# Weight sums of a seven-product up-projection taken out of its loop, with a reordered product chain

## The chip, the cores and the metric

The kernel runs on one core of one Trainium2 chip. The core has five instruction streams that run on their own: TensorE (PE, with its weight loads listed as PEld), VectorE (DVE), ScalarE (ACT), GpSimd (POOL) and SyncE (SP), the last of which only issues transfers here. The metric is the device time of one execution in microseconds, as the median of several runs.

## The reference, cut to what matters

One layer of a streaming encoder over 2048 prompt tokens and 64 sample tokens, all in float32 with `D_MODEL = 1024` and `D_FF = 2816`:

```
x  = x + rms_norm(token_mixer(rms_norm(x)))        # gated convolution and mLSTM heads
x  = x + rms_norm(memory_attend(rms_norm(x)))      # 4 heads, 256 memory tokens
up, ff_new = causal_dwconv(rms_norm(x) @ w_up, ff_buf, ffn_conv_w)    # w_up: 1024 x 5632
a, g = split(up, 2)                                # each 2816 wide
x  = x + rms_norm((gelu(g) * a) @ w_down)
```

The results are `x` and the new states; among them `new_ffn_conv`, the last two rows of `rms_norm(x) @ w_up` of the prompt and of the sample (2 x 5632 numbers each).

## The kernel before, in words

Every float32 product is made of three matmuls on TensorE: an operand is split into a rounded high part and the remainder (`split`, lines 101 and 102: ACT writes the high part as a cast, DVE subtracts it from the source), and `mm3` (lines 115 to 117) adds high-high, high-low and low-high in PSUM. The five phases run one after another; a compile-time planner orders the instructions of each engine by simulated readiness, except on the engines named in `manual_schedule`, where the written order holds. In phases 3 to 5 this is PE.

**Attention stage (`phase3`, main loop from line 1142).** Sixteen chunks of 128 tokens. One iteration issues, in this order on PE: the scores of chunk i+1 (two halves), the transposes of the normalised result of chunk i-1 (`x2_T`, line 1184, whose DVE copies `xg` go to the DRAM tensor `x2Td`), the transposes of chunk i+2, the output product of chunk i in two halves (`yout`), and between them the transposes of the softmax of chunk i+1 (`pT`, line 1067). The residual `xr` of `yout` is loaded from DRAM into a tile with one buffer. After a chunk's output, `post` and `x2n` normalise it on ACT, DVE and POOL. The three `raw` buffers of 4 KB per partition are nearly unused in this loop.

**Up-projection stage (`phase4`, from line 1191).** Tokens go in 3 passes of 704, held as four quarter matrices R11, R12, R21, R22 (half of the 1024 rows by 352 tokens). In each pass a loop runs over 22 units; unit f makes the 128 columns f of the half `a` and the 128 columns f of the half `g`. As a 2 x 2 block product this would be eight block products; the kernel makes seven (the Winograd form of Strassen's scheme) out of sums of token quarters (T1 to T4, made once a pass) and sums of weight quarters (s14, s23, made in each unit). A block product is 12 matmuls of 128 x 352, so a unit is 84. In each unit:

- SP loads two weight blocks of 512 KB (`raw`, `wr`); POOL makes four sums of 128 x 512 from them (lines 1260, 1261, 1262, 1265); ACT and DVE split the operands wa (1024 columns), wb (1024), wc (1024) and wd (512) of the next unit.
- PE makes the products in the order wa·B11, wb·T2, wb·T3, wa·B21, wc·T1, wd·T4, wc·B22. The partial sums u2 and u3 are added on DVE (lines 1398, 1404); `cg` and `ca` collect the two column blocks (lines 1412, 1418, 1423, 1431). wa·B21 is accumulated onto wa·B11's PSUM bank, and wc·B22 onto wc·T1's, the latter after DVE has read wc·T1 (line 1418).
- `conv` (lines 1346 and 1348) runs the three taps on ACT and DVE, ACT applies gelu, DVE multiplies (line 1438), and POOL stores the result in the DRAM tensor `hd`. POOL also copies the two halo columns in front of each block and behind it (lines 1324, 1326, 1351, 1353, 1354).

When a pass ends, seven token operands (B11, B21, B22, T1 to T4; one buffer each, 128 x 1408) are split anew, each after its last product of the old pass. After the last unit, two transfers on SP write the halo columns out, `self.dma(self.o["ffc"][:, :, 0], halo)` and the same for `halos`, into an output of shape (128, 44, 2, 2): each run of consecutive numbers in DRAM is two floats long.

**Down-projection (`phase5`).** `load_h` loads `hd` back (tile `hr`, split to `hh`), the weights are split to `dh` and `dl`, and PE starts on line 115 with the tile `y`.

Of the kernel before, what the change touches and what calls it, by code (L numbers as in the profile page):

```python
# [7 lines left out]
F32 = mybir.dt.float32  # L8
# [6 lines left out]
P = 128  # L15
# [50 lines left out]
class Prog:  # L66
# [68 lines left out]
    def build(self):  # L135
        tc, nc = self.tc, self.nc
        with ExitStack() as es:
# [23 lines left out]
            self.hd = dt([NF, P, T], F32, name="hd")  # L161
            self.qT = dt([4, P, T], F32, name="qTd")
# [811 lines left out]
    def phase3(self):  # L974
# [8 lines left out]
        with ExitStack() as es:  # L983
# [67 lines left out]

            zq = self.zq = self.pool(self.qes, "zq", side="right")
# [69 lines left out]

            def yout(s):
                yos = []
                xr = zq.tile([P, D], F32, tag="xr", name="xr", bufs=1)
                self.dma(xr, self.x1[s.c * P:(s.c + 1) * P])
                for nh in range(2):
# [8 lines left out]
                    if nh == 1:  # L1136
                        self.post(wk, yos, self.gb3, xr, self.x2[s.c * P:(s.c + 1) * P], yn=self.yn3,
                                  junk=s.pp[:, 0:2].rearrange("p h m -> p (h m)"))
                        x2n(self.yn3, xr)
                        todo.append((xr, s.c * P, P))  # L1140
                    yield

            todo = self.x2todo = []
            ch = {0: xT(0)}
# [4 lines left out]
            for i in range(16):  # L1149
                g = score(ch[i + 1]) if i + 1 < 16 else iter(())  # L1150
                next(g, None)
                if i == 0:
                    pT(ch[0])
                next(g, None)
                while todo:
                    self.x2_T(pt_, "tp", *todo.pop(0))
# [3 lines left out]
                next(y)  # L1160
                next(y)
                if i + 1 < 16:
                    pT(ch[i + 1])
                next(y)
                next(y)
                if i == 1:
# [7 lines left out]
                    todo.append((xt, NP_TOK, W))  # L1174

# [14 lines left out]
    def phase4(self):  # L1190
# [6 lines left out]

        tc, nc, a = self.tc, self.nc, self.a
        V, G = nc.vector, nc.gpsimd
# [4 lines left out]
        with ExitStack() as es:  # L1204
# [13 lines left out]


            ops = {n: t_op(n) for n in ("B11", "T2")}  # L1220
            raws = {n: t_raw(n) for n in ("R11", "R12", "R21", "R22")}
            wa0 = left.tile([P, 2, KT, P], F32R, tag="wa", name="wa0", bufs=1)
            wb = left.tile([P, 2, 2, KH, P], F32R, tag="wb", name="wb", bufs=1)
            X = early.tile([P, KH, NB], F32, tag="X", name="X", bufs=1)
            s23 = early.tile([P, 2, KH, P], F32, tag="s23", name="s23", bufs=1)
            s14 = early.tile([P, 2, KH, P], F32, tag="s14", name="s14", bufs=1)
            zq2 = self.zq
            halo = right.tile([P, 2 * NF, 2], F32, name="halo")
            halos = right.tile([P, 2 * NF, 2], F32, name="halos")
            G.memset(halo, 0.0)  # L1230
            self.dma(halos, a["sffn"])
# [6 lines left out]
            def w_load(u):  # L1238
                w = W()
                f = units[u][1]  # L1240
                w.r0 = self.raw(a["w_up"][f], (P, KT, P))
                w.r1 = right.tile([P, KT, P], F32, tag="wr1", name="wr1", bufs=2)
                self.dma(w.r1, a["w_up"][NF + f])
                return w

            def w_a(u, w):
                if u == 0:
                    w.a = wa0
                else:
                    w.a = (right if u % 2 else left).tile([P, 2, KT, P], F32R, tag="wa", name="wa", bufs=1)  # L1250
                self.split(w.a[:, 0], w.a[:, 1], w.r0)

            def w_s123(u, w):
                if u == 0:
                    w.s14, w.s23 = s14, s23
                else:
                    w.s14 = early.tile([P, 2, KH, P], F32, tag="s14", name="s14", bufs=1)
                    w.s23 = early.tile([P, 2, KH, P], F32, tag="s23", name="s23", bufs=1)
                a11, a21, a22 = w.r0[:, 0:KH], w.r1[:, 0:KH], w.r1[:, KH:KT]
                G.tensor_tensor(out=w.s14[:, 0], in0=a21, in1=a22, op=ALU.add)  # L1260
                G.tensor_tensor(out=w.s23[:, 0], in0=w.s14[:, 0], in1=a11, op=ALU.subtract)
                G.tensor_tensor(out=w.s23[:, 1], in0=a11, in1=a21, op=ALU.subtract)

            def w_s4(w):
                G.tensor_tensor(out=w.s14[:, 1], in0=w.r0[:, KH:KT], in1=w.s23[:, 0], op=ALU.subtract)

            def w_b(u, w):
                w.b = wb if u == 0 else left.tile([P, 2, 2, KH, P], F32R, tag="wb", name="wb", bufs=1)
                self.split(w.b[:, 0], w.b[:, 1], w.s23)

            def w_c(w):
                w.c = left.tile([P, 2, 2, KH, P], F32R, tag="wc", name="wc", bufs=1)
                self.split(w.c[:, 0], w.c[:, 1], w.s14)

            def w_d(w):
                w.d = left.tile([P, 2, KH, P], F32R, tag="wd", name="wd", bufs=1)
                self.split(w.d[:, 0], w.d[:, 1], w.r1[:, KH:KT])
# [26 lines left out]
            def t_t3(p, t):  # L1304
                V.tensor_tensor(out=t.r["R11"], in0=t.X, in1=t.r["R11"], op=ALU.subtract)
                t_split(p, t, "T3", t.r["R11"])

            def t_t4(p, t):
                V.tensor_tensor(out=t.X, in0=t.X, in1=t.r["R21"], op=ALU.subtract)
                t_split(p, t, "T4", t.X)  # L1310

            def prod(pt, wh, wl, o, more=False):
                self.mm3(pt[:, :NB], [(wh[:, k], wl[:, k], o[:, k, 0], o[:, k, 1]) for k in range(KH)],
                         first=not more, more=more)
# [4 lines left out]
            def vt(n):  # L1319
                return left.tile([P, NB], F32, tag=n, name=n, bufs=1)  # L1320

            def cbuf(j, p, n):
                c = left.tile([P, 2 * NB + 4], F32, tag=n, name=n, bufs=1)
                G.tensor_copy(c[:, 0:2], halo[:, j])
                if p == NPASS - 1:
                    G.tensor_copy(c[:, NPL + 2:NPL + 4], halos[:, j])
                return c
# [14 lines left out]
            def conv(j, p, c, n, bufs):  # L1342
# [7 lines left out]
                if p < NPASS - 1:  # L1350
                    G.tensor_copy(halo[:, j], c[:, 2 * NB:2 * NB + 2])
                else:
                    G.tensor_copy(halo[:, j], c[:, NPL:NPL + 2])
                    G.tensor_copy(halos[:, j], c[:, 2 * NB + 2:2 * NB + 4])
                return d, e


            tk = t_load(0)
            w = w_load(0)
            t_split(0, tk, "B11", tk.r["R11"])  # L1360
            w_a(0, w)
            t_adds(tk)
            w_s123(0, w)
            t_split(0, tk, "T2", tk.X)
            w_b(0, w)
            t_t3(0, tk)
            t_split(0, tk, "B21", tk.r["R21"])
            w_s4(w)
            t_split(0, tk, "T1", tk.r["R12"])
            w_c(w)  # L1370
            t_t4(0, tk)
            w_d(w)
            t_split(0, tk, "B22", tk.r["R22"])
            ws = {0: w, 1: w_load(1)}
            nt = None
            for u, (p, f) in enumerate(units):
                w, n = ws.pop(u), ws.get(u + 1)
                if u + 2 < len(units):
                    ws[u + 2] = w_load(u + 2)
# [6 lines left out]
                pa = ptile()  # L1386
                prod(pa, w.a[:, 0, 0:KH], w.a[:, 1, 0:KH], o["B11"])
                p1 = vt("p1")
                nc.scalar.copy(p1, pa[:, :NB])
                if last:  # L1390
                    t_split(p + 1, nt, "B11", nt.r["R11"])
                if n:
                    w_s123(u + 1, n)
                    w_a(u + 1, n)
# [240 lines left out]
```

## Time and profile before

| | |
|---|---|
| median of 3 runs | 3039.05 us (3037.79 to 3041.55) |
| profiled execution | 3042.33 us, of it 3040.6 us span |
| granted clock of TensorE, mean over the span | 0.974 of 2.4 GHz |
| attention loop | about 1074 to 1488 us |
| up-projection, first to last matmul | 1491.7 to 2473 us |
| down-projection, first matmul to the end | 2527.7 to 3040.6 us |

How to read it: the span is the time from the first to the last instruction; the profiled execution lies 3.3 us above the median of the timed runs. Times below are microseconds from the start of the span. A bracket at the end of a timeline row gives how long the engine was idle just before the instruction, and what released it.

### The profile page before, as it was taken

The numbers are of one execution on the slowest core, as the hardware profiler recorded it, in microseconds if no ns is written. First come the engines' busy times: TensorE is split into PE (matmuls) and PEld (weight loads), VectorE is DVE, ScalarE is ACT, GpSimd is POOL, SyncE is SP. The second block draws the span as 40 slices with busy tenths as digits, with TensorE's granted clock in tenths as the row PEclk, the third lists the DMA queues.
The fourth block names the chain that finished last, engine by engine and source line by source line (L and its number), as shares of the span: only waits on it lengthen the run. The fifth ranks groups of instructions, "written<-read, shape, count | busy, mean of one in ns | idle before, by whom it ended". The sixth has DMA issues, their size and how long they took to land.

```text
span 3040.6 us, 41676 instructions
## 1 busy us (share of the span) xinstructions
PE 2873.7 (95%) x15906; PEld 2645.1 (87%) x15906; DVE 1856.3 (61%) x2771; ACT 1121.8 (37%) x1979; POOL 1057.6 (35%) x1177
## 2 busy tenths in 40 slices
PE   8999999999999999999689998999899957999998
PEld 8999999998888777888589997999899956888887
DVE  5313421446665544444589999999999951444449
ACT  5233223235443533333344554455444423211113
POOL 1111111112212201111368786778688830000016
PEclk9999999999999999999899998999899978999999
DMA  8434232258665423222432323232222374222126
GB/s 272 142 107 134 92 107 86 69 169 291 218 210 163 141 71 104 84 84 84 141 108 96 110 102 117 101 107 98 87 101 94 106 41 103 78 78 83 51 73 216
DMA packets 172042, 358.78 MB, mean 118 GB/s; under 512 B 31046, under 2 KB 96776, under 8 KB 171842
## 3 DMA queue, kind: packets, MB, share of 16 engines
q1 hardware_dynamic: 149666, 279.63, 30.7%
q0 software_dynamic: 22176, 76.48, 6.8%
q8 instruction: 125, 2.05, 0.3%
q14 instruction: 75, 0.61, 0.1%
HBM read 270.58 MB, written 85.47 MB: 117 GB/s over the span
## 4 chain that ended last, share of the span: by engine, by line
PE 45%; DVE 12%; issue 5%; ACT 2%; SPq 1%; DMA 1%; POOL 0%; DVEq 0%; ACTq 0%; POOLq 0%
PE up L115 6%; PE up L116 6%; PE up L117 6%; PE y L116 4%; PE y L117 4%; PE y L115 4%; DVE da L1348 2%; PE yo L116 2%; PE yo L117 2%; PE yo L115 2%; PE sc L117 2%; PE sc L115 2%; PE sc L116 2%; DVE acc L566 1%; SPq L71 1%
## 5 line engine op out<-in xcount | busy, mean ns | idle before, releaser
L115 PE MATMUL y<-dh,hh 128*128 128x512 f32 x704 | 275.0, 391 | 54.2 <-ACT dh L101 54.2
L116 PE MATMUL y<-dl,hh 128*128 128x512 f32 x704 | 275.0, 391 | 0.5 <-DVE dl L102 0.5
L117 PE MATMUL y<-dh,hh 128*128 128x512 f32 x704 | 274.9, 390 | 0.0
L115 PE MATMUL mm<-xs,wh 128*128 128x384 f32 (+2 forms) x768 | 249.6, 325 | 10.2 <-ACT xs L107 7.5
L117 PE MATMUL mm<-xs,wl 128*128 128x384 f32 (+2 forms) x768 | 249.4, 325 | 1.3 <-DVE wl L102 1.3
L116 PE MATMUL mm<-xs,wh 128*128 128x384 f32 (+2 forms) x768 | 249.0, 324 | 0.0
L1534 DVE TENSOR_TENSOR acc<-y,acc 128x512 f32<-128x512 f32 x170 | 115.5, 689 | 181.2 <-PE y L117 180.4
L115 PEld LDWEIGHTS y<-dh,hh 128*128 128x128 f32 x704 | 132.8, 189 | 82.2 <-ACT dh L101 54.5
L115 PE MATMUL up<-T,wb 128*128 128x352 f32 x528 | 172.6, 327 | 9.7 <-ACT wb L101 9.7
L1348 DVE SCALAR_TENSOR_TENSOR da<-ca,cst,da 128x704 f32<-128x704 f32 (+1 forms) x132 | 174.5, 1322 | 9.1 <-ACT da L1346 9.0
L115 PE MATMUL up<-B,wa 128*128 128x352 f32 x528 | 174.5, 330 | 3.0 <-ACT B L101 3.0
L116 PE MATMUL up<-B,wa 128*128 128x352 f32 x528 | 172.6, 327 | 3.0 <-DVE B L102 3.0
L115 PE MATMUL mmb<-bh,xs 128*128 128x384 f32 (+1 forms) x512 | 173.4, 339 | 0.0
L117 PE MATMUL up<-B,wa 128*128 128x352 f32 x528 | 172.6, 327 | 0.0
L117 PE MATMUL up<-T,wb 128*128 128x352 f32 x528 | 171.0, 324 | 1.7 <-DVE wb L102 1.7
L117 PE MATMUL mmb<-bh,xs 128*128 128x384 f32 (+1 forms) x512 | 172.5, 337 | 0.0
L116 PE MATMUL mmb<-bl,xs 128*128 128x384 f32 (+1 forms) x512 | 172.4, 337 | 0.0
L116 PE MATMUL up<-T,wb 128*128 128x352 f32 x528 | 170.9, 324 | 0.0
L560 POOL TENSOR_TENSOR fo<-fo,gpost 64x512 f32<-64x512 f32 x2 | 2.5, 1282 | 465.8 <-ACT junk L556 465.8
L101 ACT CAST hh<-hr 128x1024 fp32r<-128x1024 f32 (+3 forms) x54 | 49.5, 916 | 311.3 <-PE y L117 262.1
L116 PEld LDWEIGHTS y<-dl,hh 128*128 128x128 f32 x704 | 132.6, 188 | 28.5 <-DVE dl L102 1.2
L117 PEld LDWEIGHTS y<-dh,hh 128*128 128x128 f32 x704 | 132.7, 189 | 27.9 <-DVE hh L102 0.5
(458 smaller groups left out, 8637.8 us busy)
## 6 DMA issues: line engine op xcount, KB each, us to landing
raw<-in_w_up SPq DMA_DIRECT2D x66, 512.0 KB, 3.4
wr<-in_w_up SPq DMA_DIRECT2D x66, 512.0 KB, 3.3
raw<-in_wA SPq DMA_DIRECT2D x47, 512.0 KB, 3.6
xt<-in_x SPq DMA_DIRECT2D x32, 512.0 KB, 4.7
hr<-hd SPq DMA_DIRECT2D x32, 512.0 KB, 3.8
hd<-da POOLq DMA_DIRECT2D x44, 352.0 KB, 3.2
kvo_t<-kvo SPq DMA_DIRECT2D x16, 770.0 KB, 5.6
braw<-in_wB SPq DMA_DIRECT2D x64, 192.0 KB, 3.3
```

Source lines behind the costliest of these rows:

```text
L71: self.nc.sync.dma_start(out=out, in_=in_)
L101: nc.scalar.copy(hi, src)
L115: nc.tensor.matmul(out, lhsT=lh, rhs=rh, start=(first and i == 0), stop=False, skip_group_check=more)
L116: nc.tensor.matmul(out, lhsT=lh, rhs=rl, start=False, stop=False, skip_group_check=more)
L117: nc.tensor.matmul(out, lhsT=ll, rhs=rh, start=False, stop=(last and i == n - 1), skip_group_check=more)
L560: (nc.gpsimd if pg else nc.vector).tensor_tensor(out=yn[:w, cut[i]], in0=h, in1=gb[:w, cut[i]], op=ALU.mult)
L566: nc.vector.scalar_tensor_tensor(out=yn[:w, sl], in0=yn[:w, sl], scalar=r[:w, 0:1], in1=xt[:w, sl], op0=ALU.mult, op1=ALU.add)
L1348: V.scalar_tensor_tensor(out=d[:, :e], in0=c[:, i:e + i], scalar=w[i], in1=d[:, :e], op0=ALU.mult, op1=ALU.add)
L1534: V.tensor_tensor(out=acc[j][:, sl], in0=pt, in1=acc[j][:, sl], op=ALU.add)
```

## The change

Sums of weight quarters are made for each of the 22 column blocks once, in the attention loop, by DVE: 44 calls of the generator `sums`, each with four loads, four DVE instructions and one store into a new DRAM tensor `wsd`. The up-projection loads the sums back. In the unit the products are reordered: three further products are accumulated onto the first one's bank, ACT copies the bank at each partial sum, and the first two products of a unit (`head1`, `head2`) are issued among the last ones of the unit before. ACT makes the small halo copies instead of POOL. In the attention loop SP keeps the written order, and in the last iteration the transposes of chunk 14 stand behind the first half of the output product; chunk 15 uses `s.x` as its residual. The output `ffc` becomes (2, 128, 88), so that a partition's halo columns lie together, and `halos` is loaded in unit 1.

```
+            es.enter_context(tc.manual_schedule(engines={mybir.EngineType.SP}))   # phase3 loop
+            def sums():
+                for f in range(NF):
+                    for q in range(2):
+                        t = self.rawp.tile([P, 4, 2 * P], F32, tag="raw", name="sums", bufs=3)
+                        for i, j in ((0, f), (1, NF + f)):
+                            src = a["w_up"][j].rearrange("p (two k) c -> p two k c", two=2)[:, :, 2 * q:2 * q + 2]
+                            for h in range(2):
+                                self.dma(t[:, i + 2 * h], src[:, h].rearrange("p k c -> p (k c)"))
+                        a11, a21, a12, a22 = (t[:, i] for i in range(4))
+                        V.tensor_tensor(out=a22, in0=a21, in1=a22, op=ALU.add)
+                        V.tensor_tensor(out=a21, in0=a11, in1=a21, op=ALU.subtract)
+                        V.tensor_tensor(out=a11, in0=a22, in1=a11, op=ALU.subtract)
+                        V.tensor_tensor(out=a12, in0=a12, in1=a11, op=ALU.subtract)
+                        self.store(self.wsd[f, :, :, q * 2 * P:(q + 1) * 2 * P], t)
+                        yield
...
+                if i != 1:
+                    next(ws, None)          # before the second half of the scores
-                while todo:
+                while todo and i < 15:
                     self.x2_T(pt_, "tp", *todo.pop(0))
...
                 next(y)
+                next(ws, None)
                 next(y)
+                while todo:
+                    self.x2_T(pt_, "tp", *todo.pop(0))
...
                 next(y)
+                if i > 1:
+                    next(ws, None)
                 next(y)
```

In the up-projection (the new unit, cut to its order):

```
+                w.r["wa"] = self.raw(a["w_up"][f], (P, KT, P)).rearrange("p (two k) c -> p two k c", two=2)
+                for n, i in (("wb", 0), ("wc", 2)):
+                    w.r[n] = early.tile([P, 2, KH, P], F32, tag="ws", name="ws", bufs=3)
+                    self.dma(w.r[n].rearrange("p i k c -> p i (k c)"), self.wsd[f, :, i:i + 2])
+                w.r["wd"] = right.tile([P, KH, P], F32, tag="wr1", name="wr1", bufs=2)
+                self.dma(w.r["wd"], a["w_up"][NF + f][:, KH:KT])
...
+            def head1(u, w, o):
+                prod(v.a, w, "wa", 0, o["B11"])
+                nc.scalar.copy(v.p1, v.a[:, :NB])
+            def head2(v, o):
+                prod(pb, v.w, "wa", 1, o["B21"])
+                v.ca = cbuf(v.f, v.p, "ca", 2)
+                put(v.ca, v.p, 0, lambda d, sl: V.tensor_tensor(out=d, in0=pb[:, sl], in1=v.p1[:, sl], op=ALU.add))
...
+                prod(v.a, w, "wb", 0, o["T2"], more=True)
+                nc.scalar.copy(u2, v.a[:, :NB])
+                w_split(n, "wc")
+                prod(pc, w, "wc", 1, o["T1"])
+                prod(v.a, w, "wb", 1, o["T3"], more=True)
+                nc.scalar.copy(u3, v.a[:, :NB])
+                cg = cbuf(NF + f, p, "cg", 1)
+                put(cg, p, 1, lambda d, sl: V.tensor_tensor(out=d, in0=pc[:, sl], in1=u3[:, sl], op=ALU.add))
+                w_split(n, "wb")
+                vn = head1(u + 1, n, on) if n else None
+                prod(v.a, w, "wd", None, o["T4"], more=True)
+                put(cg, p, 0, lambda d, sl: nc.scalar.copy(d, v.a[:, sl]))
+                w_split(n, "wd")
                 dg, e = conv(NF + f, p, cg, "dg", 1)
                 nc.scalar.activation(dg[:, :e], dg[:, :e], AF.Gelu_apprx_tanh)
+                if n:
+                    head2(vn, on)
+                w_split(ws[u + 2], "wa")
+                prod(pc, w, "wc", 0, o["B22"], more=True)
+                put(v.ca, p, 1, lambda d, sl: V.tensor_tensor(out=d, in0=pc[:, sl], in1=u2[:, sl], op=ALU.add))
...
-            self.dma(self.o["ffc"][:, :, 0], halo)
-            self.dma(self.o["ffc"][:, :, 1], halos)
+            for i, t in enumerate((halo, halos)):
+                self.dma(self.o["ffc"][i], t.rearrange("p j t -> p (j t)"))
```

At the last unit of a pass the splits of B11, B21 and T2 stand behind the first product, T1 behind the second, T3 behind the third, T4 behind the gelu and B22 behind the last. wa has one buffer (before, two in turn), wc has two.

## Rows read from the trace of the kernel before

**Rows 1.** The page: busy time, share of the span and instructions of each engine.
```profile
PE 2873.7 (95%) x15906; PEld 2645.1 (87%) x15906; DVE 1856.3 (61%) x2771; ACT 1121.8 (37%) x1979; POOL 1057.6 (35%) x1177
```
**Rows 2.** Windows: stretch, length, busy time (count) by engine, granted clock, DMA, GB/s.
```profile
1200.00:1300.00 100.00, 99.72 (x482) 82.22 (x481) 44.31 (x97) 32.15 (x80) 13.81 (x21) 1.00 0.26 85
1600.00:1700.00 100.00, 100.00 (x620) 99.09 (x619) 94.51 (x102) 50.31 (x66) 80.42 (x68) 1.00 0.29 102
2505.00:2510.00 5.00, 0.00 (x0) 0.00 (x0) 0.00 (x0) 0.00 (x0) 0.00 (x0) 0.50 1.28 1
```
**Rows 3.** Timeline of PE, attention's end and unit 0: start, length, instruction, idle before.
```profile
1474.71 1.94 PE L1184 MATMUL tp<-ident,xr 128*128 128x128 f32 x8 [6.95 <-DVE xr L1121]
1488.26 0.39 PE L117 MATMUL yo<-B,ps 128*128 128x512 f32 x1
1508.38 0.66 PE L115 MATMUL up<-T,wb 128*128 128x352 f32 x1 [9.70 <-ACT wb L101]
1530.91 0.32 PE L115 MATMUL up<-B,wa 128*128 128x352 f32 x1
```
**Rows 4.** Timeline of ACT: the copy behind each unit's first product, units 1 to 65.
```profile
1533.06 0.45 ACT L1389 COPY p<-up 128x352 f32<-128x352 f32 x1
...
1582.76 0.43 ACT L1389 COPY p<-up 128x352 f32<-128x352 f32 x1
...
1814.69 0.43 ACT L1389 COPY p<-up 128x352 f32<-128x352 f32 x1
...
1904.03 0.43 ACT L1389 COPY p<-up 128x352 f32<-128x352 f32 x1
...
2135.80 0.43 ACT L1389 COPY p<-up 128x352 f32<-128x352 f32 x1
...
2194.30 0.43 ACT L1389 COPY p<-up 128x352 f32<-128x352 f32 x1
...
2463.26 0.43 ACT L1389 COPY p<-up 128x352 f32<-128x352 f32 x1
```
**Rows 5.** Waits from 1510 to 2480: total, times, longest.
```profile
PE up L115 <- DVE cg L1418: 39.5, 28, 8.0
```
**Rows 6.** Groups by shape, 1530 to 2420: count, busy, mean ns, idle before.
```profile
L102 DVE TENSOR_TENSOR wb<-s,wb 128x1024 fp32r<-128x1024 f32 x61 | 96.4, 1581 | 0.0
L102 DVE TENSOR_TENSOR wc<-s,wc 128x1024 fp32r<-128x1024 f32 x62 | 75.4, 1217 | 0.0
L1348 DVE SCALAR_TENSOR_TENSOR dg<-cg,cst,dg 128x704 f32<-128x704 f32 x88 | 83.2, 946 | 8.3 <-ACT dg L1346 8.3
L1438 DVE TENSOR_TENSOR da<-da,dg 128x704 f32<-128x704 f32 x44 | 80.1, 1820 | 1.2
```
**Rows 7.** Timeline of DVE in two places where POOL was idle.
```profile
1493.41 1.62 DVE L102 TENSOR_TENSOR B<-R,B 128x1408 fp32r<-128x1408 f32 x1
2465.68 0.90 DVE L1438 TENSOR_TENSOR da<-da,dg 128x706 f32<-128x706 f32 x1
```
**Rows 8.** Waits from 2470 to 2545.
```profile
PE y L115 <- ACT dh L101: 54.2, 1, 54.2
```
**Rows 9.** Timelines of SP and ACT between up- and down-projection.
```profile
2476.07 8.13 SPq L71 DMA_DIRECT2D out_ffc<-halos  x1
2484.37 26.17 SPq L71 DMA_DIRECT2D hr<-hd  x2
...
2523.71 0.83 ACT L101 CAST hh<-hr 128x768 fp32r<-128x768 f32 x1 [46.79 <-DMA hr<-hd]
```
**Rows 10.** The page: packets by size.
```profile
DMA packets 172042, 358.78 MB, mean 118 GB/s; under 512 B 31046, under 2 KB 96776, under 8 KB 171842
```
**Rows 11.** Timelines of DVE and PE in attention: softmax of chunk 15, its transposes.
```profile
1458.09 0.69 DVE L1109 TENSOR_TENSOR pp<-pp,sm 128x512 f32<-128x512 f32 x1
...
1461.28 1.03 PE L1067 MATMUL tp<-ident,pp 128*128 128x128 f32 x8
```
**Rows 12.** DMA issues: size of each, median us from issue to landing.
```profile
x1t<-x1d SPq DMA_DIRECT2D x15, 512.0 KB, 3.5
hd<-da POOLq DMA_DIRECT2D x44, 352.0 KB, 3.2
```

More of the change, by code (lines that the diff above doesn't have):

```diff
@@ L1174, in phase3 @@
                     todo.append((xt, NP_TOK, W))
+            for _ in ws:
+                pass
     def x2_T(self, pp, tag, xn, t0, w):
@@ L1238, in w_load @@
             def w_load(u):
+                if u >= len(units):
+                    return None
                 w = W()
+                w.u = u
                 f = units[u][1]
-                w.r0 = self.raw(a["w_up"][f], (P, KT, P))
-                w.r1 = right.tile([P, KT, P], F32, tag="wr1", name="wr1", bufs=2)
-                self.dma(w.r1, a["w_up"][NF + f])
-                return w
-            def w_a(u, w):
-                if u == 0:
-                    w.a = wa0
-                else:
-                    w.a = (right if u % 2 else left).tile([P, 2, KT, P], F32R, tag="wa", name="wa", bufs=1)
-                self.split(w.a[:, 0], w.a[:, 1], w.r0)
@@ L1253, in w_s123 @@
[L1253 to L1277, printed above, removed]
+                w.r = {}
@@ new lines, in w_load, with w_split @@
+                w.o = {}
+                return w
+            def w_split(w, n):
+                if w is None:
+                    return
+                if n == "wd":
+                    o = left.tile([P, 2, KH, P], F32R, tag="wd", name="wd", bufs=1)
+                else:
+                    o = first.pop(n, None)
+                    if o is None:
+                        o = w_op(n, 2 if n == "wc" else 1)
+                self.split(o[:, 0], o[:, 1], w.r[n])
+                w.o[n] = o
@@ L1317, in ptile, with vt, cbuf @@
                 return pu.tile([P, 512], F32, tag="up", name="up")
[L1319 to L1324, printed above, removed]
+            def vt(n, bufs=1):
+                return left.tile([P, NB], F32, tag=n, name=n, bufs=bufs)
+            def cbuf(j, p, n, bufs):
+                c = left.tile([P, 2 * NB + 4], F32, tag=n, name=n, bufs=bufs)
+                nc.scalar.copy(c[:, 0:2], halo[:, j])
                 if p == NPASS - 1:
-                    G.tensor_copy(c[:, NPL + 2:NPL + 4], halos[:, j])
+                    nc.scalar.copy(c[:, NPL + 2:NPL + 4], halos[:, j])
                 return c
@@ L1395, in phase4 @@
-                pb = ptile()
-                prod(pb, w.b[:, 0, 0], w.b[:, 1, 0], o["T2"])
-                u2 = vt("u2")
-                V.tensor_tensor(out=u2, in0=pb[:, :NB], in1=p1, op=ALU.add)
-                if last:
+                    for x, y in (("B11", "R11"), ("B21", "R21")):
+                        t_split(p + 1, nt, x, nt.r[y])
                     t_split(p + 1, nt, "T2", nt.X)
                 pc = ptile()
-                prod(pc, w.b[:, 0, 1], w.b[:, 1, 1], o["T3"])
-                u3 = vt("u3")
@@ L1404, in phase4 @@
-                V.tensor_tensor(out=u3, in0=pc[:, :NB], in1=u2, op=ALU.add)
-                if n:
-                    w_b(u + 1, n)
-                    w_s4(n)
-                if last:
-                    t_t3(p + 1, nt)
-                prod(pa, w.a[:, 0, KH:KT], w.a[:, 1, KH:KT], o["B21"], more=True)
-                ca = cbuf(f, p, "ca")
-                put(ca, p, 0, lambda d, sl: nc.scalar.copy(d, pa[:, sl]))
-                if last:
-                    t_split(p + 1, nt, "B21", nt.r["R21"])
```

117 lines of the change are left out of this document (59 added, 58 removed).

## The prediction

> **What bounds the kernel now.** I read the page's busy shares first, then the windows, then what PE waited for. PE is busy 95% of the span [rows 1], so only its idle time and its slow-clock time can be won; the number of matmuls stays the same (84 in a unit). The windows show where this holds: in the attention loop PE is at 99.7 of 100 us while DVE works 44.3; in the up-projection PE and DVE are both full (100.0 and 94.5) and POOL works 80.4 [rows 2]. There the reader is to see two engines side by side at the limit. The pace of the units, read from the copy that ACT makes behind each unit's first product [rows 4], tells what that costs:
>
> - units 3 to 20 follow each other at (1814.69 - 1582.76) / 17 = 13.64 us: PE's own pace, 84 matmuls at 0.162;
> - units 1 to 3 lose 49.70 - 3 x 13.64 = 8.8;
> - the first change of pass loses 89.34 - 5 x 13.64 = 21.1, the second 58.50 - 3 x 13.64 = 17.6, together 38.7;
> - in the last pass 19 units take 268.97, that is 14.16 each, 9.8 too much.
>
> In these stretches the waits name one line: PE waits 39.5 us in total, up to 8.0 at once, for DVE's read of wc·T1 (`cg`, line 1418) before it may accumulate wc·B22 on that bank [rows 5]. The cause is DVE's backlog, not that instruction. Two larger holes lie outside. Between the end of the attention stage (1488.26 + 0.39) and the start of unit 1 (1530.91) stand 42.3 us for a unit that needs 13.6: 28.6 lost; the longest single wait in it, 9.7, is for wb, which is cast from POOL's chain of sums [rows 3]. Before it PE waits 6.95 for the normalised chunk 14 [rows 3]. And between up- and down-projection PE waits 54.2 [rows 8]. All of these add up to 147 us, and that is the most that can be won.
>
> **The change part by part.**
>
> *The gap of 54.2.* The two halo transfers move 2 x 128 x 44 = 11,264 packets of two floats, a third of all packets under 512 B [rows 10]. SP needs 8.13 us to issue the second one; the load `hr` behind it is issued at 2484.37 and its data are cast at 2523.71, 39.3 us later, while such loads land in 3 to 4 [rows 9, 12]; in this time the DMA engines are busy at a share of 1.28 and move 1 GB/s [rows 2]. The new layout makes 256 packets of 352 B. What is late next: halo copies on ACT behind the last product (about 3 us, bounded by a DVE eviction and ACT copies of at most 0.45 each [rows 4]), two short issues (1), `hr` (3.5), and from the first cast to the first matmul 4.0 as now (2523.71 to 2527.7). That is 11.5; I take 12, so 42 won. Ends: 30, if the second `hr` waits for the halo tiles to be written out, and 50, if `hr` is issued ahead.
>
> *Unit 0.* POOL's chain of sums goes, wb and wc are loaded. What is late next is DVE and the tiles that lie where the attention stage still works: the splits of B21 and T3 can't begin before its last products and its last normalisation. Seven token splits and four token sums of about 1.62 [rows 7] and the splits wa, wb, wc, wa of 1.22 and wd of 0.6 [rows 6] are 23.3 us of DVE, against 9 products of 1.95 = 17.5 for PE (head1 and head2 of unit 1 are among them); some 12 of the 23 can be done before the attention stage ends, since the sources are loaded without waiting behind `xr` of chunk 15. I leave 9 lost of 28.6 and 3 of the 8.8 in units 1 to 3: 20 + 6 won, between 11 and 33.
>
> *Attention's end.* Twenty-four of the last 48 matmuls move in front of the transposes of chunk 14. PE was free at 1474.71 - 6.95 = 1467.8; half of the 12 us from the transposes to 1488.3 puts the transposes at 1473.8, and their data come at 1474.7: 6 won, between 0 and 8.
>
> *Changes of pass.* DVE per unit is 94.5% of 13.64 = 12.9 now [rows 2, 4]. With POOL's two-input work gone I price DVE's instructions at what they take when POOL is idle: a wb split at 1.22 as wc has it (now 1.58), the final product 0.90 (now 1.82), a tap 0.95 [rows 6, 7]. After: three splits of 1.22, one of 0.6, three PSUM reads of 0.5 (five before), four taps, one product: 3.7 + 0.6 + 1.5 + 3.8 + 0.9 = 10.5. A change of pass adds seven splits and two sums of 1.62 = 14.6. Two units then need 2 x 10.5 + 14.6 = 35.6 of DVE against 27.3 of PE; B11 and B21 are free a unit earlier and take up that unit's 3.1 of slack. Some 5 remain for each change, 10 of 38.7: 28 won. If the order holds the splits back, 10; if the backlog is covered by the longer lead of the products, 36.
>
> *The last pass.* At 10.5 (11 with the cut evictions there) DVE is under PE's 13.64, so the 9.8 go: 10 won, at least 4.
>
> *ACT in the unit.* It works 50.3% of 13.64 = 6.9 [rows 2]. Added are two PSUM copies of 0.45 [rows 4] and four to eight halo copies of two columns, which no row shows on ACT: above nothing, below 0.45, I take 0.2. That makes 8.6 to 9.4 of 13.64. It lies beside PE only as long as each copy is made within the one product (1.95) that stands between two sums on the bank. I charge 2 for the 66 units, with ends of 0 and 20. What stands behind a late copy on ACT are the weight casts.
>
> *The sums in the attention loop.* 44 calls of four DVE instructions of 128 x 256, which no row shows; a 512-column one takes 0.69 [rows 11], so 0.35 to 0.69, and I take 0.4 (nearer the half). Three calls in a chunk of 25 us (120 matmuls and transposes of 482 in 100 us [rows 2]) add 4.8 to 11.1 of DVE: room enough, since 55.7% of DVE is free there. Of the chains that PE waits for, the tightest has the softmax ready at 1458.78 for transposes at 1461.28 [rows 11], 2.5 of slack, and a call that gets in between costs 1.6. The four loads of a call stand in SP's written order with `x1t`, the store on POOL's queue with the small powers of the norms; a raw buffer is back after some 3.5 + 1.6 + 3.2 us [rows 12] and three are wanted in 25. I charge 4 for the stage, the later first load included; ends 0 and 25. The Trainium skill speaks against it (SBUF — State Buffer, section SBUF: two separate sides): a transfer issued by GpSimd has its descriptors written on GpSimd's cores, which are locked out while VectorE runs a two-port instruction, so the stores would starve. Here the trace doesn't bear it out: the `hd` stores of the same kind land in 3.2 us beside a DVE that is 94.5% busy [rows 2, 12]; by the row the stores cost nothing, by the rule raw buffers would return late and the 25 would be due.
>
> **The sum.** 42 + 26 + 6 + 28 + 10 - 2 - 4 = 106. Against the profiled execution's 3042.3 this gives 2936; that execution lies 3.3 above the median, so 2933 for the runs. With all lower ends 30 + 11 + 0 + 10 + 4 - 20 - 25 = 10 (3029), with all upper ends 50 + 33 + 8 + 36 + 10 = 137 (2902).
>
> **The rivals.**
>
> *DVE stays behind at the changes of pass and in unit 0.* For it: splits wait for the last use of a tile with one buffer, and ACT and DVE take instructions in a fixed order, so one that waits holds all behind it. Against it: 3 us of slack per unit that weren't there. It would leave 20 of the 28 and 12 of the 26 unwon: 2965. Chance 0.17.
>
> *The gap isn't the packets'.* Then `hr` waits for something else, a tile or the last store of `hd`, and the 42 are missing: 2975. Against it: the DMA share of 1.28 at 1 GB/s with no other work queued [rows 2]. The Trainium skill would give this rival a ground (DMA: Bandwidth & Descriptors, section Why small descriptors are slow): a packet costs a fixed three or so cycles beside its bytes, which for 11,264 packets on 16 engines at its 850 MHz is an estimate of 3 us, not 39. The trace of before disagrees by a factor of ten. Chance 0.05.
>
> *PE is tied to ACT.* Three sums go onto a bank that ACT has to read in between. If ACT waits at the head of its queue, for a tap that DVE hasn't fed or for gelu, the copy comes late and PE stops in every unit. For it: before, only DVE's line 1418 stood in such a place, and it was the one that cost 39.5 [rows 5]. Against it: ACT is 65% busy and has 1.95 - 0.45 = 1.5 us of cover each time. The point from which it decides: PE has to lose (106 + 2) / 66 = 1.6 us in each unit to make up for all else. With two copies late by 1.2 beyond their cover it is 2.4 x 66 = 158 lost: 3089, slower. Chance 0.04.
>
> *The stage runs still better than forecast*: unit 0 and the changes of pass nearly whole, the gap at a few us: 2908. Chance 0.12.
>
> **How the numbers follow.** The forecast has 0.62, the rivals 0.17, 0.05, 0.04 and 0.12. The predicted time is the likeliest case's, 2933. The range leaves out the slower rival and the far ends of both sides: 2902 to 2978. About 0.2% (6 us) is what a measurement can tell from no change here; the chances are faster 0.95, same 0.01, slower 0.04.
>
> **What would show it.** In the profile after: the first matmul of the down-projection within 8 to 16 us of the last of the up-projection, and fewer than 20,000 packets under 512 B; units 13.6 us apart in all three passes; DVE near 77% in the up-projection and a final product of 0.9; two changes of pass with 3 to 8 us each beyond the pace; POOL nearly empty there; DVE at 60 to 65% in the attention loop with chunks still 25 us apart. Wrong would be: chunks longer than 25.3 us, PE waits on ACT's u2 or u3, or a gap above 30 us with the packets gone.

## The result, and the profile after

The changed kernel takes 2935.2 us (median of 4, 2933.1 to 2937.4) beside 3040.3 for the kernel before: a ratio of 0.966 (95% interval 0.964 to 0.967), 105 us faster. The forecast was 2933. The sum came out right, but not all of its terms did; two were too high and two too low, and they cancelled.

The profiled execution took 2936.1 us, its span is 2934.4, so it is compared with the 3042.3 and 3040.6 of before. First the page, busy time and packets, as [rows 1, 10]:

```profile
PE 2845.4 (97%) x15906; PEld 2628.5 (90%) x15906; DVE 1716.7 (59%) x2815; ACT 1205.4 (41%) x2463; POOL 380.5 (13%) x605
...
DMA packets 211580, 456.33 MB, mean 156 GB/s; under 512 B 25654, under 2 KB 113912, under 8 KB 211378
```

POOL fell from 1057.6 to 380.5 us, ACT rose by 84. The windows that answer to [rows 2] (length, busy time and count by engine, granted clock, DMA share, GB/s), and the start of the up-projection:

```profile
1200.00:1300.00 100.00, 99.71 (x481) 82.22 (x480) 61.77 (x144) 31.94 (x81) 21.27 (x33) 1.00 0.63 210
...
1489.50:1504.10 14.60, 0.03 (x1) 0.00 (x0) 6.73 (x10) 6.41 (x11) 1.82 (x4) 0.57 0.73 255
1504.10:1510.00 5.90, 4.00 (x12) 3.34 (x12) 5.85 (x4) 2.19 (x3) 0.00 (x0) 0.61 1.06 382
1510.00:1515.00 5.00, 1.53 (x4) 1.15 (x5) 4.54 (x4) 4.89 (x5) 0.00 (x0) 0.71 0.83 269
1515.00:1526.00 11.00, 11.00 (x59) 11.00 (x58) 10.04 (x9) 5.44 (x6) 0.00 (x0) 0.82 0.61 203
1526.00:1554.00 28.00, 27.39 (x174) 27.09 (x173) 24.57 (x30) 17.24 (x31) 2.04 (x3) 1.00 0.67 218
...
1600.00:1700.00 100.00, 100.00 (x626) 100.00 (x625) 76.30 (x91) 59.54 (x112) 3.78 (x7) 1.00 0.50 163
```

Attention has PE as full as before with DVE at 61.8 instead of 44.3. In the up-projection DVE came down from 94.5 to 76.3, and PE, which was called full at 620 matmuls in 100 us, now makes 626. In between PE does nothing for 14.6 us, and the granted clock is 0.57 there, 0.61 and 0.71 in the next 11 us and only 0.82 in the 11 us after them, in which PE is busy all the time again. These are means of two levels, 1.2 and 2.4 GHz: unit 0's matmuls start 0.29 us apart from 1506.25 to 1508.60 and, after a second idle stretch of 3.07 us, again from 1514.59 to 1518.70; from 1518.98 on they start 0.16 apart.

PE's timeline at the places of [rows 3, 8] (start, length, idle before and what ended it):

```profile
1481.34 1.94 PE L1217 MATMUL tp<-ident,xr 128*128 128x128 f32 x8 [6.29 <-DVE xr L1123]
...
1504.13 0.66 PE L115 MATMUL up<-B,wa 128*128 128x352 f32 x1 [14.61 <-ACT B L101]
...
1512.21 0.66 PE L115 MATMUL up<-B,wa 128*128 128x352 f32 x1 [3.07 <-ACT B L101]
...
2421.99 0.79 PE L115 MATMUL y<-dh,hh 128*128 128x512 f32 x1 [9.40 <-ACT dh L101]
```

The 54.2 ahead of the down-projection are 9.4. The 6.95 ahead of chunk 14's transposes are still 6.29, and a wait of 14.6 stands where 3.0 and 9.7 stood. What held these two up shows on DVE (a sum that waits for its load, ahead of chunk 14's norm), on SP (the load of the token halves) and on ACT (the first token cast):

```profile
1478.18 0.43 DVE L1136 TENSOR_TENSOR sums<-sums 128x256 f32<-128x256 f32 x1 [3.65 <-DMA sums<-in_w_up]
...
1494.36 5.24 SPq L71 DMA_DIRECT2D R<-x2Td  x4
...
1502.71 1.36 ACT L101 CAST B<-R 128x1408 fp32r<-128x1408 f32 x1 [3.77 <-DMA R<-x2Td]
```

ACT's copy behind head1 of units 4, 22, 23, 44, 45, 46 and 65, as [rows 4]:

```profile
1568.28 0.46 ACT L1385 COPY p<-up 128x352 f32<-128x352 f32 x1 [0.44 <-PE up L117]
...
1810.92 0.46 ACT L1385 COPY p<-up 128x352 f32<-128x352 f32 x1 [0.53 <-PE up L117]
...
1826.98 0.46 ACT L1385 COPY p<-up 128x352 f32<-128x352 f32 x1 [0.49 <-PE up L117]
...
2110.06 0.46 ACT L1385 COPY p<-up 128x352 f32<-128x352 f32 x1 [0.53 <-PE up L117]
...
2126.12 0.46 ACT L1385 COPY p<-up 128x352 f32<-128x352 f32 x1 [0.39 <-PE up L117]
...
2140.30 0.46 ACT L1385 COPY p<-up 128x352 f32<-128x352 f32 x1 [0.26 <-PE up L117]
...
2396.42 0.46 ACT L1385 COPY p<-up 128x352 f32<-128x352 f32 x1 [0.35 <-PE up L117]
```

Units follow each other at (1810.92 - 1568.28) / 18 = 13.48 us. The changes of pass lose 16.06 - 13.48 = 2.6, and 2.6 + 0.7 (14.18 - 13.48). The wait of [rows 5] and the groups of [rows 6], after:

```profile
PE up L115 <- DVE cg L1442: 1.8, 3, 0.7
```
```profile
L102 DVE TENSOR_TENSOR wb<-ws,wb 128x1024 fp32r<-128x1024 f32 x64 | 78.4, 1225 | 22.5 <-ACT wb L101 22.5
...
L1465 DVE TENSOR_TENSOR da<-da,dg 128x704 f32<-128x704 f32 x44 | 39.2, 891 | 1.3
```

A copy in the new order finds two products (24 matmuls, 3.85 us) fewer behind it than the same copy before; the ledger corrects for that.

Each row is a stretch of the span in us; "won" is before less after.

| from, to | before | after | won | forecast |
|---|---|---|---|---|
| start, attention's last matmul | 1488.6 | 1489.5 | -0.9 | 6 - 4 |
| then, unit 4's first product | 94.1 | 82.6 | 11.5 | 26 |
| then, unit 65's first product | 880.5 | 828.1 | 52.4 | 28 + 10 - 2 |
| then, first matmul of y | 64.4 | 21.7 | 42.7 | 42 |
| the rest | 512.9 | 512.4 | 0.5 | 0 |

### The profile page after: what moved, and what is told of

Its sections match the earlier page's. It is cut to its first block, busy times and chain, and to the rows that moved or that the text cites. A ratio compares the mean times of both kernels' runs of the same rounds, so it can differ in the third digit from the quotient of the medians.

```text
span 2934.4 us, 41883 instructions
## 1 busy us (share of the span) xinstructions
PE 2845.4 (97%) x15906; PEld 2628.5 (90%) x15906; DVE 1716.7 (59%) x2815; ACT 1205.4 (41%) x2463; POOL 380.5 (13%) x605
## 2 busy tenths in 40 slices
DMA packets 211580, 456.33 MB, mean 156 GB/s; under 512 B 25654, under 2 KB 113912, under 8 KB 211378
## 4 chain that ended last, share of the span: by engine, by line
PE 55%; DVE 5%; issue 2%; DMA 2%; ACT 1%; POOL 0%; SPq 0%; DVEq 0%; POOLq 0%; ACTq 0%
PE up L115 10%; PE up L117 10%; PE up L116 10%; PE y L116 4%; PE y L117 4%; PE y L115 4%; PE yo L115 2%; PE yo L117 2%; PE sc L117 2%; PE sc L115 2%; PE sc L116 2%; PE yo L116 2%; DVE acc L567 1%; DMA sums<-in_w_up 1%; DVE acc L1563 1%
## 5 line engine op out<-in xcount | busy, mean ns | idle before, releaser
L74 POOL DMA_DIRECT2D hd<-da x88 | 47.4, 541 | 868.0 <-DVE da L1465 827.2
L117 PEld LDWEIGHTS y<-dh,hh 128*128 128x128 f32 x704 | 132.6, 188 | 27.8 <-DVE hh L102 0.5
L115 PEld LDWEIGHTS mm<-xs,wh 128*128 128x128 f32 x768 | 145.9, 190 | 10.2 <-ACT xs L107 7.7
```

The costliest lines, as they stand in the source:

```text
L74: self.nc.gpsimd.dma_start(out=out, in_=in_)
L115: nc.tensor.matmul(out, lhsT=lh, rhs=rh, start=(first and i == 0), stop=False, skip_group_check=more)
L117: nc.tensor.matmul(out, lhsT=ll, rhs=rh, start=False, stop=(last and i == n - 1), skip_group_check=more)
```

## The experiments

Times are medians with their lowest and highest; each was run beside the kernel before, and the ratio is to that.

**The gap: the halo layout alone.** Theory: 11,264 packets of 8 B are the gap. Rival: `hr` waits for something else.
```
 before.py
-  self.dma(self.o["ffc"][:, :, 0], halo); self.dma(self.o["ffc"][:, :, 1], halos)
+  for i, t in enumerate((halo, halos)):
+      self.dma(self.o["ffc"][i], t.rearrange("p j t -> p (j t)"))
```


> The kernel before with nothing but the halo output laid out contiguously. If the gap of 54.2 us between up- and down-projection is the 11,264 packets of 8 bytes: the gap falls to about 12, packets under 512 B by some 11,000, the time by about 42 to 2997 to 3000. If the gap is a tile that comes free late or another transfer: the gap stays above 45 and the time within 8 us of 3040.

2995.7 us (2994.8 to 2997.2), ratio 0.986 (0.984 to 0.987): 44 won. Its page's packets and its wait ahead of y:
```profile
DMA packets 161034, 358.78 MB, mean 120 GB/s; under 512 B 20038, under 2 KB 85768, under 8 KB 160834
```
```profile
L115 PE MATMUL y<-dh,hh 128*128 128x512 f32 x704 | 275.2, 391 | 9.4 <-ACT dh L101 9.4
```
11,008 packets fewer (11,264 less 256), and the same 9.4 as with the whole change. The theory holds and the rest of the change has no part in it.

**The start: token halves read first.** Theory: the 14.6 come from SyncE's order, which reads `R` behind the first weights (issued at 1494.36). Rival: another engine's order.
```
+  with tc.manual_schedule(engines={mybir.EngineType.SP}):
       tk = t_load(0)
       w = w_load(0)
```


> The changed kernel, with SP loading the four token quarters ahead of the weights at the start of the up-projection. If PE's wait of 14.6 us there is SP's order (the token loads stand behind a weight-sum load that waits for the residual tile of chunk 15): the wait for B11 falls under 3 and the time by 10 to 16, to about 2922. If the tokens wait for their own space or for bandwidth: the wait stays above 10 and the time within 4 of 2935.

2932.6 us (2931.1 to 2933.1), ratio 0.965 (0.963 to 0.966): 2.6 below the changed kernel, which is less than can be told. `R` is issued at 1472.52 now, but the first product still waits 14.66, for the cast of wa. ACT's timeline:
```profile
1490.20 0.60 ACT L557 ACTIVATE pp<-yo 128x512 f32<-128x512 f32 x1 [13.89 <-PE yo L117]
...
1494.06 1.06 ACT L1121 ACTIVATE xr<-yn 128x1024 f32<-128x1024 f32 x1 [3.17 <-DVE yn L567]
...
1496.26 0.19 ACT L1342 COPY ca<-halo 128x2 f32<-128x2 f32 x1 [1.05 <-POOL halo L1263]
...
1496.55 2.62 ACT L101 CAST B<-R 128x1408 fp32r<-128x1408 f32 x2
1501.14 1.36 ACT L101 CAST T<-R 128x1408 fp32r<-128x1408 f32 x1 [1.96 <-DVE R L1318]
1502.41 1.36 ACT L101 CAST B<-R 128x1408 fp32r<-128x1408 f32 x1
1503.67 1.04 ACT L101 CAST wa<-raw 128x1024 fp32r<-128x1024 f32 x1
```
The theory's time fell. In the changed kernel the load of `R` was indeed the last thing missing (ACT stands idle for 3.77 us until it lands, above), but with it early the wait is as long as before. The sources are there; ACT is in front of them. Its order has chunk 15's two norms first, then the copies of the zero halo, which the change moved to ACT and which wait for POOL's memset, then casts for later products, and wa last. That isn't the written order: in the code wa's split stands first, but only PE's order (here SP's too) is held as written, and the planner put wa's cast last.

**The pace: GpSimd works beside.** Theory: before, POOL's sums made VectorE's two-input instructions longer, and that, not PE, set pace and backlog. Rival: it was the number of VectorE's instructions.
```
   (the changed kernel, four additions in each unit whose result nobody reads)
+  for i in range(4):
+      nc.gpsimd.tensor_tensor(out=scr, in0=n.r["wd"], in1=scr, op=ALU.add)
```


> The changed kernel, with four additions of 128 x 512 on GpSimd in each unit whose result nobody reads. If the gain in the loop comes from VectorE running without GpSimd's two-input work: VectorE's wb split goes back from 1.2 to about 1.5 us and the final product from 0.9 towards 1.8, VectorE's share from about 78% to over 88%, the two changes of pass lose 5 us more each and the time is 2945 to 2965. If the gain comes from the order of the products: VectorE may slow down, but the units stay at 13.48 and the time within 4 of 2935.

2974.1 us (2972.9 to 2977.4), ratio 0.978 (0.977 to 0.980): 39 slower than the changed kernel. The same instructions as in [rows 6], grouped from 1830 to 2100:
```profile
L102 DVE TENSOR_TENSOR wb<-ws,wb 128x1024 fp32r<-128x1024 f32 x20 | 36.0, 1800 | 0.0
L1470 DVE TENSOR_TENSOR da<-da,dg 128x704 f32<-128x704 f32 x19 | 33.8, 1781 | 0.6
```
The final product is back at 1.78 from 0.89, wb at 1.80 from 1.23, and DVE is busy 262.8 of 270 us (208.2 without the additions). Which instructions pay shows in one unit: four additions run from 1914.62 to 1921.60, and the taps of `dg`, which begin behind them, keep their length.
```profile
1914.62 6.98 POOL L1433 TENSOR_TENSOR scr<-wr,scr 128x512 f32<-128x512 f32 x4 [6.02 <-DMA wr<-in_w_up]
...
1923.28 0.95 DVE L1368 SCALAR_TENSOR_TENSOR dg<-cg,cst,dg 128x704 f32<-128x704 f32 x1
```
The changes of pass lose 36 us: 22.1 + 18.6 + 16.7 + 15.3 + 14.7 less 5 x 13.48 is 20.0, the second one 16.0; before it was 38.7. So the backlog is GpSimd's doing, and the effect was larger than expected. For the pace the theory fell: from unit 27 (copy at 1907.52) to unit 43 (2123.50) the units are 13.50 apart, with DVE that full; only in the last pass are they 13.64. The Trainium skill (SBUF — State Buffer, section SBUF: two separate sides) says that a VectorE instruction with two SBUF inputs and a GpSimd instruction that reads SBUF exclude each other for their whole length; the doubled 0.89 agrees with that.

**The order: sums from DRAM, products as before.** Theory: most of the changes of pass goes with POOL's work, the new order of the products adds less. Rival: the order does it.
```
   (the changed kernel; the seven products in the order of before, wa in two buffers instead of wc)
...
-  prod(v.a, w, "wb", 0, o["T2"], more=True);  nc.scalar.copy(u2, v.a[:, :NB])
+  prod(pb, w, "wb", 0, o["T2"]);  V.tensor_tensor(out=u2, in0=pb[:, :NB], in1=p1, op=ALU.add)
-  prod(v.a, w, "wb", 1, o["T3"], more=True);  nc.scalar.copy(u3, v.a[:, :NB])
+  prod(pc, w, "wb", 1, o["T3"]);  V.tensor_tensor(out=u3, in0=pc[:, :NB], in1=u2, op=ALU.add)
...
```


> The changed kernel with the sums from DRAM, but with the product order, the banks and the buffers of wa and wc of the kernel before. If the sums' removal from the loop makes the gain: units at 13.48 to 13.55 in all passes, changes of pass at 4 to 9 us each, time 2940 to 2955. If the longer chain and the interleaved products make it: changes of pass at 12 us or more each, a pace above 13.6, time 2960 to 2985.

2947.0 us (2945.9 to 2948.1), ratio 0.969 (0.968 to 0.971): 12 slower than the changed kernel. The first change of pass:
```profile
1804.20 0.43 ACT L1425 COPY p<-up 128x352 f32<-128x352 f32 x1
...
1826.14 0.45 ACT L1425 COPY p<-up 128x352 f32<-128x352 f32 x1
...
1839.05 0.43 ACT L1425 COPY p<-up 128x352 f32<-128x352 f32 x1
...
1852.12 0.44 ACT L1425 COPY p<-up 128x352 f32<-128x352 f32 x1
...
1865.79 0.43 ACT L1425 COPY p<-up 128x352 f32<-128x352 f32 x1
```
It loses 1865.79 - 1804.20 - 4 x 13.48 = 7.7 and the second 8.6, 16.3 together; elsewhere the units are 13.49 apart. So of 38.7, the sums' leaving takes 22.4 and the order, on top of it, 10.4. The two don't simply add: with the new order and GpSimd's additions the run before still loses 36, so the order alone wins little there. The slower pace of before came back in neither run's first two passes; by these two runs it took the old order and GpSimd's additions together.

**Sums finished earlier.**
```
                 next(ws, None)
+                if 1 < i < 6:
+                    next(ws, None)
```


> Two more steps of the weight sums are taken in the chunks 2 to 5 of attention, so that all 44 are made by chunk 14 and none stands between the last two chunks. Theory: in the changed kernel the last step of the sums stands on DVE ahead of the normalization of chunk 14 and waits 3.65 us for its load, and TensorE's wait ahead of the transposes of that chunk grew to 6.29 us by this; with the step gone the wait falls to about 2.5 us and the up-projection starts 3 to 4 us earlier: 2930 to 2933 us against 2935.2. Rival: the first product waits for casts on ACT whose token halves are read late (1494), so what attention's end wins is lost ahead of that product: 2934 to 2937. A second rival, DVE is too full in chunks 2 to 5 for two more steps each (about 1.7 us each): chunks of over 26 us there, 2937 to 2942.

2933.2 us (2931.4 to 2935.1), ratio 0.965 (0.963 to 0.966): no change that can be told. The wait ahead of chunk 14's transposes fell to 1.51, but the chunks 2, 3 and 5 grew. ACT's first instruction of chunks, from which their lengths are read (33.68, 26.53, 25.03, 27.36):
```profile
1139.89 1.06 ACT L1093 ACTIVATE pp<-x1t 128x1024 f32<-128x1024 f32 x1
...
1173.57 1.06 ACT L1093 ACTIVATE pp<-x1t 128x1024 f32<-128x1024 f32 x1
...
1200.10 1.06 ACT L1093 ACTIVATE pp<-x1t 128x1024 f32<-128x1024 f32 x1
...
1225.13 1.06 ACT L1093 ACTIVATE pp<-x1t 128x1024 f32<-128x1024 f32 x1
...
1252.49 1.06 ACT L1093 ACTIVATE pp<-x1t 128x1024 f32<-128x1024 f32 x1
```
In the changed kernel they are 31.64, 25.02, 25.03, 25.01. What was won at the end, 4.8, was paid in the middle, 5.9: the second rival's longer chunks, with the first theory's shorter wait.

**The sums' additions left out** (loads and stores stay).
```
-  V.tensor_tensor(out=a22, in0=a21, in1=a22, op=ALU.add)     (and the three others)
```


> The loads and stores of the weight sums stay, the 176 additions on VectorE (0.42 us each, 74 us in all) are left out, so the operands that the up-projection reads are not sums. It prices the moved additions at their new place. Theory (TensorE sets attention, DVE has room): the period of a chunk stays 25.02 us; gained are only the 2 us lost in chunks 2 to 4 and some 3 to 4 us ahead of chunk 14's transposes: 2929 to 2935 us. Rival, the additions delay each chunk's softmax or normalization a little: 0.3 us or more in each of 14 chunks, 2925 or less, chunks of 24.7 or less. Rival, loads and stores (not the additions) cost what attention lost: no change, 2934 to 2937.

2936.4 us (2932.9 to 2944.1), ratio 0.966 (0.964 to 0.968): no change that can be told, the last rival. Chunks stay at 25.02 with DVE at 44.4 of 100 us. The wait ahead of chunk 14's transposes is even 7.11: with no addition to wait, the store waits for the loads, on POOL's queue, and the norm's power stands behind it:
```profile
1472.91 0.71 POOL L74 DMA_DIRECT2D wsd<-sums  x1 [5.52 <-DMA sums<-in_w_up]
1473.57 0.64 POOL L95 TENSOR_TENSOR por<-pov,small 128x1 f32<-128x1 f32 x1
```
So the 176 additions cost nothing that can be told; what costs, by these two waits, is an instruction that waits for its own load ahead of the norm, on whichever queue.

**The start mended**, three parts at once (sums early as above, too): `R11` and the first weight tile are read first, the halves in the order of their products, the first halo copies are back on GpSimd.
```
-  nc.scalar.copy(c[:, 0:2], halo[:, j])
+  (nc.gpsimd.tensor_copy if p == 0 and j % NF < 2 else nc.scalar.copy)(c[:, 0:2], halo[:, j])
...
-  for n in ("R11", "R12", "R22", "R21"):
+  for n in ("R11", "R21", "R12", "R22") if p == 0 else ("R11", "R12", "R22", "R21"):
...
```


> A candidate: sums early as in the run beside it; SyncE reads the first token half before all weights, then the first weight tile, then the other halves in the order of their products; the three copies of the zero halo of units 0 and 1 are back on GpSimd. Theory (the hole ahead of the first product is ACT's written order: casts of later weights and halo copies stand ahead of the first token cast): ACT casts the first token half right behind the last norm of attention, the wait of the first product falls from 14.6 us to 6 to 9, units 0 to 3 win 6 to 10 us, and 3 from the sums: 2921 to 2928. Rival, the remaining casts and splits of unit 0 (some 12 us of ACT, as much of DVE) bound the first products whatever their order: the holes move to the second and third product, 2929 to 2933.

2927.7 us (2925.5 to 2929.6), ratio 0.963 (0.961 to 0.964): the theory, at its upper end, and something of the rival: waits of 3.51 and 2.03 us, for wb and T2, now stand in the third product. (The order that the expectation calls ACT's written one is the planner's, as said above.) With B21 beside B11 in place of T2:

> As the run beside it, but the second token operand (B21) has a place of its own beside the first one's and T2 takes the place that overlays attention's buffers. Theory: if the second product waits for a buffer of attention, it starts earlier here: up to 3 us below the run beside it. Rival: it waits for the cast itself, and nothing changes (within 1.5 us of the run beside it).

2926.1 us (2924.6 to 2932.7), ratio 0.963 (0.960 to 0.965): not to be told from the run beside it. Its first product:
```profile
1494.75 0.66 PE L115 MATMUL up<-B,wa 128*128 128x352 f32 x1 [7.36 <-ACT wa L101]
```
The wait is halved, as expected; what remains is chunk 15's norm, which ACT still has ahead of the first cast.

**Sums spread, and the changed kernel beside.** The extra steps in chunks 7 and 11, or 4, 7, 9 and 11.

> The version with B21 in its own place, but the sums are taken ahead by one extra step in chunks 7 and 11 only, instead of one in each of chunks 2 to 5. Theory: in chunks 2, 3 and 5 the extra step stalled VectorE on its own load and made these chunks 2.0, 1.5 and 2.3 us longer, which ate what the shorter wait ahead of chunk 14's transposes gave; two steps later on cost at most 2 us each: 2921 to 2926 us, 9 to 14 below the changed kernel run beside it. Rival: the extra step costs the same 2 us in any chunk and the sums' last step still stands in chunk 15's way: 2926 to 2929.

2929.2 us (2928.2 to 2931.3), ratio 0.964 (0.963 to 0.965).

> The same with the four extra steps in chunks 4, 7, 9 and 11, so that no sum is made in the last chunk. Theory: as the run beside it within 2 us, the chunk lengths show 25.0 except where the extra step waits for its load (27). Rival: each extra step costs 2 us: 4 us slower than the run with two.

2938.5 us (2933.2 to 2940.7), ratio 0.967 (0.965 to 0.968).

> The changed kernel itself on the same chip as these two, so that they are compared with it directly: 2933 to 2937 us.

2935.3 us (2934.1 to 2938.1), ratio 0.966 (0.965 to 0.967). On one chip the version with two steps is 6 us below the changed kernel, and no run of one lies among the other's. But the expectation of the spread steps fell: a late step costs more, not less. With two, the chunks that hold them are 29.3 and 30.0 us long, and in the first DVE waits for the extra step's load:
```profile
1292.20 1.06 ACT L1093 ACTIVATE pp<-x1t 128x1024 f32<-128x1024 f32 x1
...
1321.49 1.06 ACT L1093 ACTIVATE pp<-x1t 128x1024 f32<-128x1024 f32 x1
```
```profile
1296.77 0.43 DVE L1136 TENSOR_TENSOR sums<-sums 128x256 f32<-128x256 f32 x1 [3.81 <-DMA sums<-in_w_up]
```
With four, their chunks are 26.6, 29.7, 28.8 and 27.8 long. Three steps in a chunk leave it at 25.0, a fourth mostly does not. Why it costs 0 to 2.3 us in chunks 2 to 5 and up to 5 later wasn't separated.

**The start alone** (the sums where the change put them; the order of the loads, the place of B21 and the first halo copies as in the run with B21 above).

> The changed kernel with the order of the start alone mended (first token half read first, B21 in its own place, the first halo copies on GpSimd); the sums stand where the change put them, so no chunk is longer for them. Theory: the chunks stay at 25.0 us, the wait ahead of chunk 14's transposes stays at 5 to 6 us, the first product comes 7.4 us behind attention's last instead of 14.6, and units 0 to 3 win 6 to 7 us: 2927 to 2931. Rival: the start is bound by the work of ACT and VectorE in unit 0 and the 7 to 9 us of the other versions came from the sums made early: 2933 to 2936.

2929.1 us (2925.6 to 2932.1), ratio 0.963 (0.962 to 0.964): the theory. From chunk 3 on chunks are at 25.0, and PE's timeline shows the short wait, with the long one of attention still there, at 8.16 even longer than the 5 to 6 expected:
```profile
1483.12 1.94 PE L1217 MATMUL tp<-ident,xr 128*128 128x128 f32 x8 [8.16 <-DVE xr L1123]
...
1499.13 0.66 PE L115 MATMUL up<-B,wa 128*128 128x352 f32 x1 [7.36 <-ACT wa L101]
```
From attention's last matmul (1491.77) to the copy in unit 4 (1564.48) it takes 72.7 us instead of 78.8, so 6.1 of the missing 14.5 are back. Which of the three parts brought it wasn't separated. The versions with the mended start, at 2926 to 2929, lie 6 to 9 us below the changed kernel, all but the one with four late steps (2938.5); only that one and the one with two were run beside it on one chip, and which version is best can't be told.

## Why the prediction was right, and where not

- *The gap*: 42 forecast, 42.7 measured, 44 by itself. The cause was read right: 1.28 DMA share at 1 GB/s [rows 2].
- *Unit 0*: the step that failed. "Some 12 of the 23 can be done before the attention stage ends, since the sources are loaded without waiting behind `xr` of chunk 15" was wrong twice. The sources weren't loaded early (`R` at 1494.36, behind `ws`; SP waits 8.0 us there for DVE's last read of `x1t`, which the change keeps in use for chunk 15), and where they were, in the run with the token halves first, ACT's order held their casts behind chunk 15's norms and wa's behind the others. The forecast counted instructions on DVE and never asked in which order the planner would put ACT's. 11.5 came instead of 26. A second part of it is clock: after the hole many matmuls of unit 0 start 0.29 us apart and not 0.16. Before, the clock was low there too, 0.63 to 0.66 from 1491.6 to 1530, and with the hole halved (the start alone) it still is, 0.52 in the first 5.9 us; that 20 won would have needed the hole closed is argued from this, not shown.
- *Attention's end*: 6 forecast, about nothing came with the stage as a whole at -0.9. From chunk 15's softmax transposes (1463.12, before 1461.28) to attention's last matmul it takes 26.4 us instead of 27.4: the matmuls moved as forecast, but "their data come at 1474.7" was wrong. A step of the sums, which waits 3.65 for its load, was put by the planner ahead of chunk 14's norm, and the data came at 1481.2. I had asked what a step costs that gets between softmax and transposes (1.6), not what a step costs that waits. Another 2 us went in chunk 2 (31.64, before 29.61).
- *Changes of pass*: 28 forecast, 32.8 measured (38.7 to 5.9). The price of DVE's instructions without POOL was right (1.225, 0.891, 0.947 for 1.22, 0.90, 0.95), and DVE at 76.3 beside the forecast 77.
- *The last pass*: 10 forecast, 9.8.
- *The pace*: missing from the sum. I called 13.64 "PE's own pace"; it is 13.48, 84 at 0.1605, and 61 units make 9.8 of it. The rest was the same read of wc·T1 that costs 39.5 in [rows 5], too short at a time for PE's busy share: from 1600 to 1790 of the kernel before, the weight loads wait for it in every second unit, 2.3 us for 14 units, or 0.16 each:
```profile
PEld up L115 <- DVE cg L1418: 2.3, 7, 0.6
```
[Rows 2] had the sign of it: 620 matmuls in a window that says 100.0 busy, with PEld at 99.09. (The 17 steps behind the 13.64 are those from unit 4 to unit 21, not units 3 to 20; the sum stands.)
- *ACT in the unit*: 2 forecast, nothing visible; it works 59.5% of the pace and PE's waits on u2 and u3 are 0.5 and 0.6, once each.
- *The stores on POOL's queue*: landed in 3.6 us beside a DVE that is 62% busy, as the row of before said.
```profile
wsd<-sums POOLq DMA_DIRECT2D x44, 512.0 KB, 3.6
```
The rule weighed in the forecast speaks of two-port instructions of VectorE, and no row names those; the runs show that these stores didn't starve, and don't test the rule.
- *Packets*: fewer than 20,000 under 512 B were forecast, 25,654 came. My own figures give 31,046 - 11,264 + 256 = 20,038 (the halo layout alone has just that); the change adds 5,616, and to which of its transfers they belong I haven't found.

The errors were +14.5 and +2.9 against -16.4 and -0.7 (and 0.5 in the rest), so the total is right partly by luck: the gap, the last pass and the changes of pass were right in cause and near in size, unit 0 and attention's end were not, and the pace, which the forecast lacked, paid for most of them.

## What to carry to other kernels

When work moves across a stage boundary, read in the trace the order that every engine's queue got there, and not in the code alone, where a planner orders it: an instruction that waits for its load at the head of a queue costs more than its own length (here a sum of 0.43 us that waited 3.65 ahead of a norm), and so does a cast for a later product ahead of the first one's. Before calling a pace the bound of an engine that is 100% busy, count its instructions in a window of another variant: here PE showed 100.0 of 100 us at 620 matmuls and at 626. And count the packets of a transfer when they are of a few bytes: here 11,264 of 8 B cost 43 us.

## What the runs showed of the hardware

Additions on GpSimd made VectorE's two-input instructions that they met take up to double (the final product 0.89 to 1.78 us, the wb split 1.23 to 1.80), while the taps of one half (`dg`, 0.945) kept their length: which instruction pays is a matter of when GpSimd runs. 11,264 packets of 8 B cost 43 us; shared by 16 engines that is an estimate of 61 ns for each (43 x 16 / 11,264). And after a hole of 14.6 us, in which PE did nothing, the granted clock was 0.61, 0.71 and 0.82 in the next 5.9, 5 and 11 us, with a second idle stretch of 3.07 us among them; unit 0's matmuls started 0.29 us apart for a while after each, instead of 0.16. Here a hole cost more than its length.
